# Expert weights as 8 KB runs per partition, with strided transposes to match

## The chip, the cores and the metric

The kernel runs on one core of a Trainium2 chip. The metric is the device time of one execution in microseconds; the time before is 1277.94 us, the median of three runs from 1277.46 to 1278.04.

## The reference, cut to what matters

One encoder block over 1024 tokens of width 1024, all in float32. A token mixer (multi-scale pooling and banded attention, gated and merged) and a layer norm come first and are not touched here. Then comes a mixture of experts: a router picks one of 4 groups and then 2 of its 8 experts for each token, so 2048 token rows are spread over 32 experts. For the rows `xb` of an expert `e`:

```python
hb = jax.nn.silu(xb @ w_gate[e]) * (xb @ w_up[e])      # [rows, 512]
y  = hb @ w_down[e]                                    # [rows, 1024]
```

`w_gate[e]` and `w_up[e]` are 1024 x 512, `w_down[e]` is 512 x 1024. The rows of `y`, weighted by the router, are added up per token, and a second layer norm closes the block. A matrix product sums over its inner index, so that index may be dealt out in any order, if both factors are dealt out alike.

## The kernel before, in words

TensorE multiplies over the partition axis, 128 values of the inner index at a time. Each float32 factor is split into a high and a low part in the format `float32r`, and a product is three matmuls: high by high, high by low, low by high (`mm3`, lines 94 to 98). Weights are the streamed operand, 512 columns wide; the transposed token rows are the loaded operand.

An expert's weights come as six chunks of 1 MB: `c` = 0, 1 are the halves of gate, 2, 3 those of up, 4, 5 those of down. `load_chunk` (line 980) reads a chunk into a tile `we` with a DMA that SyncE issues (GpSimd for a few early ones, of which some lie in parts in other tiles), line 995. `w_split` (line 999) makes the high part `weh` on ScalarE (line 1005) and the low part `wel` on VectorE (line 1007). The rows of weight are dealt out by `"(k p) c -> p k c"`: partition p holds the rows p, p + 128, p + 256 and so on, so a chunk brings four separate rows of 2 KB (gate, up) or two of 4 KB (down) to each partition.

The blocks of rows are 33 and have fixed sizes: four of 128 rows, 28 of the sizes in `CAPS` (the larger experts get the larger ones), and a second block of 64 rows for the largest expert:

```python
CAPS = [128]*5 + [112, 104, 104, 96, 96, 88, 80, 80] + [72]*4 + [64]*2 + [56]*3 + [48]*3 + [40]*2 + [32]
```

For a block, `gather` (line 1159) fetches its token rows into `xin` by an indirect DMA on GpSimd's queue, up to three blocks ahead. `x_transpose` (line 1165) turns them on TensorE, eight transposes of 128 columns into `xtp` in PSUM (line 1172); ScalarE and VectorE write the high and low parts into `xinT`. `chunk` (line 1177) does the matmuls of one weight chunk. After gate and up, `hidden` makes `h` (ScalarE, VectorE), and `h_transpose` (line 1204) turns `h` with four transposes into `htp` (line 1208), evicted into `hT`. `finish` scales `y` and adds it to DRAM by an indirect DMA on GpSimd's queue.

The order is written out by hand. `SEQ` holds for each block its chunks 0 to 3, and then chunks 4 and 5 of the block before it. After chunk 3 of a block TensorE turns the next block's rows, and after the following chunk 4 it turns `h`. `run_ahead` issues loads and splits as far ahead as buffers allow: 20 large buffers (`NBIG`) are shared by loaded chunks and their split parts, and splits run three to four chunks ahead. At the 12th block from the end, `overflow_setup` (line 1108) puts some thirty small operations on VectorE (line 1116 and on).

Of the kernel before, what the change touches and what calls it, by code (L numbers as in the profile page):

```python
# [33 lines left out]
EPS = 1e-5  # L34
OVF_MAX = 40          # nine experts have less than 64 rows, every other overflow block takes at least 65 of 2048 places
FIXED = 4             # experts whose places in the order don't depend on their counts
NV = NE - FIXED
CAP_UNIT = 8
CAPS = [128] * 5 + [112, 104, 104, 96, 96, 88, 80, 80] + [72] * 4 + [64] * 2 + [56] * 3 + [48] * 3 + [40] * 2 + [32]
SECOND = 64           # rows of the largest expert's second block  # L40
RANKS = S + 128
# [8 lines left out]
def kernel(  # L50
# [50 lines left out]

# [1 line left out]
    xh = [bigtile([128, 2, S], F32R, f"xh{j}") for j in range(4)]  # L103
# [35 lines left out]
    kT = [bigtile([128, NKV, S], F32R, f"kT{a}") for a in range(2)]  # L139
    # v's parts side by side, those of the second head the other way round  # L140
    vS = bigtile([128, NT, NKV, 2, HD], F32R, "vS")
# [24 lines left out]
    def rope_apply(t, i, n, tmp, eng=pool):  # L166
        # t = t * [cos cos] + swap(t) * [-sin sin], n heads of 64
        tv = t.rearrange("p (h a d) -> p h a d", h=n, a=2)
        sv = tmp.rearrange("p (h a d) -> p h a d", h=n, a=2)
        th = t.rearrange("p (h d) -> p h d", h=n)  # L170
        for a in range(2):
            eng.tensor_mul(sv[:, :, a, :], tv[:, :, 1 - a, :],
                            rope[:, i, 1, a * 32:(a + 1) * 32][:, None, :].to_broadcast([128, n, 32]))
        eng.tensor_mul(th, th, rope[:, i, 0, :][:, None, :].to_broadcast([128, n, HD]))
        eng.tensor_add(t, t, tmp)
# [49 lines left out]
    for h in range(2):  # L225
        sp.dma_start(wq[h], w_in[h * 512:(h + 1) * 512, 512:1024].rearrange("(k p) c -> p k c", p=128))
# [1 line left out]
    oh, ol, ob = [], [], []  # L228
# [8 lines left out]
    def q_proj(i, k):  # L237
        # one contraction tile of the query projection of block i
        if k == 0:
# [60 lines left out]
    def p_transpose(n):  # L300
        # one bank for two heads' first two key blocks, one for all heads' third
        b, h = divmod(n, NH)
# [12 lines left out]
    def p_evac(b, kv, q):  # L315
        # the q-th of the banks
        k0, k1 = krange(b)
# [23 lines left out]
    def o_evac(b, kv):  # L341
        # the sum over v's parts, the low part's half moved beside the high part's
        osb = ob[0]
        hi, lo = [slice(a * HD, (a + 1) * HD) for a in ((0, 1) if kv == 0 else (1, 0))]
        act.activation(osb[hi, 2 + kv], OP[b, kv][lo], AF.Copy)
        dve.tensor_add(osb[hi, b % 2], OP[b, kv][hi], osb[hi, 2 + kv])
# [54 lines left out]
    def hl_part(key, q):  # L401
        # a quarter of it
        if q == 0:
            RAW[key], WH[key] = WH[key], bigtile([128, 2, KT, 128], F32R, "ghl")
        raw, hl = RAW[key], WH[key]
        sl = slice(2 * q, 2 * q + 2)
        split(hl[:, 0, sl], hl[:, 1, sl], raw[:, sl])
# [4 lines left out]
    def gate_fill(n, k):  # L412
        # the first gate channels, where the last blocks leave the tensor engine free
        if k == 0:
# [13 lines left out]

    # the order of the steps before the first block, in turns of eight heads
    FIRST = {  # L430
# [10 lines left out]
    }  # L441
    # the order of a block's steps, in heads from its first head's turn
    ORDER = {
# [76 lines left out]

# [1 line left out]
    pb = ExitStack()  # L522
# [28 lines left out]
    def channels(key, half):  # L551
        # one 128-channel projection, channels on partitions, 512 tokens
        ps = gpp.tile([128, 512], F32, name="gps", bufs=3)
# [33 lines left out]
    def pool_window(j):  # L587
        # u is padded by eight zero columns on either side
        u = P["u", j]
# [3 lines left out]
        for s in range(j + 1):  # L593
            dst = gp.tile([128, W2], F32, name="wsum", bufs=2)
            # windows [t - d, t + d - 1] from two halves
            a, b_ = (1, 0) if s == 0 else (d // 2, d // 2)
# [30 lines left out]
    def project(s):  # L627
        # the channels of step s, for both halves of the tokens
        kind, j = steps[s]
# [68 lines left out]
    def routing_setup():  # L698
        # the slot table starts out with unused slots, their rows after those of the tokens
        trif = bigtile([128, 2, 128], F32, "trif")  # L700
# [53 lines left out]

# [1 line left out]
    pc = ExitStack()  # L756
# [23 lines left out]
    def logit_setup():  # L780
        # logits of LN(r): rstd * (r @ (g w)) - rstd * mean * (g @ w) + b @ w + bias
        dve.tensor_copy(eio, rc[0:1, 12:44])
# [11 lines left out]
    def rstd_of(r, v, t):  # L794
        # r = v ** -0.5 by Newton's method from a bit-level first guess, each step with its sign turned
        dve.tensor_scalar(v, v, EPS, 0.5, op0=ALU.add, op1=ALU.mult)
# [80 lines left out]
    def route_a(i):  # L877
        # choices and weights of token tile i
        lg = rp_.tile([128, 36], F32, name="lg")
# [9 lines left out]
        def first(x, m, rev, scr, k, h):  # L889
            # one-hot of the first position where x reaches m  # L890
            dve.scalar_tensor_tensor(scr, x, m, rev, op0=ALU.is_ge, op1=ALU.mult)
# [28 lines left out]
    def rank(i):  # L920
        # each expert's number times 1, its tokens so far times 32
        rk = rpp.tile([128, NE], F32, name="rk", bufs=1)
# [25 lines left out]

    # experts: the first FIXED in their order, the rest by their counts, RANK[p] the place among them
    RANK = {FIXED + q: r for q, r in enumerate(list(range(1, 7)) + [0] + list(range(7, NV)))}  # L950
# [3 lines left out]
    EXP = {p: p for p in range(FIXED)}  # L954
    # blocks in their order, with the expert place that each one's weights belong to
    BLOCKS = []
# [10 lines left out]
    for b, p, c in SEQ:  # L967
        if (p, c) not in LOADS:
            LOADS.append((p, c))
    # these two wait in buffers that the first blocks don't need yet  # L970
    GA = 3
# [4 lines left out]
    W = {}  # L976
    # the last chunks come in parts, the work on them follows sooner
    CUTS = {k: 2 for k in LOADS[-4:]}

    def load_chunk(key, e, eng=sp, aside=None):  # L980
        b, c = key
        if c < 4:
            src = (w_gate, w_up)[c // 2][e].rearrange("(k p) c -> p k c", p=128)[:, 4 * (c % 2):4 * (c % 2) + 4, :]
        else:
            src = w_down[e].rearrange("(k p) c -> p k c", p=128)[:, 2 * (c - 4):2 * (c - 4) + 2, :]
        n = src.shape[1]
# [79 lines left out]

# [1 line left out]
    tabv = tabd.rearrange("(r e) c -> r e c", e=NE)  # L1068
# [16 lines left out]
    novi = const.tile([128, 1], I32, name="novi")  # L1085
    # experts by their counts, the larger ones first
    sq = [128, NV, NV]
# [12 lines left out]

# [1 line left out]
    pd = ExitStack()  # L1102
# [5 lines left out]
    def overflow_setup():  # L1108
        # places of an expert past its static blocks go by 128, (j, e) the j-th such block of expert e
        rk = rk28  # L1110
# [22 lines left out]
    def overflow_next():  # L1133
        # the next overflow block's expert and its rows of the slot table
        v = mp.tile([128, 1], F32, name="ov", bufs=1)
# [13 lines left out]
    def place(b, p):  # L1149
        # the slots of a block  # L1150
        if p < FIXED:
# [12 lines left out]

    def x_transpose(b):
        n = ROWS[b]
        XT[b] = mp.tile([128, 2, KT, 128], F32R, name="xinT", bufs=1)
        for kk in range(2):
            ps = mpp.tile([128, 4, 128], F32, name="xtp", bufs=2)
            for c in range(4):  # L1170
                k = 4 * kk + c
                pe.transpose(ps[:, c, :n], XIN[b][:n, k * 128:(k + 1) * 128], ident[:n, :n])  # L1172
            split(XT[b][:, 0, 4 * kk:4 * kk + 4, :n], XT[b][:, 1, 4 * kk:4 * kk + 4, :n], ps[:, :, :n])
# [30 lines left out]
    def h_transpose(b):  # L1204
        n = ROWS[b]
        ps = mpp.tile([128, 4, 128], F32, name="htp")
        for c in range(4):
            pe.transpose(ps[:, c, :n], H[b][:n, c * 128:(c + 1) * 128], ident[:n, :n])
        HT[b] = mp.tile([128, 2, 4, 128], F32R, name="hT")
# [26 lines left out]
    for q in range(2, FIXED):  # L1236
        place(*BLOCKS[q])
    # how far the weights may be loaded and split ahead at each step
    last = {}
# [78 lines left out]

# [1 line left out]
    lp2 = ctx.enter_context(tc.tile_pool(name="lp2", bufs=2, reuse_waits="tile"))  # L1320
# [9 lines left out]
    def stats(i0):  # L1330
        mv = lp2.tile([128, 2, 8], F32, name="mv2", bufs=4)
        MV[i0] = mv
        for q in range(2):
            r = R[i0 + q]
            if i0 + q in ACT_STATS:
                # mean, and mean square about it
                junk = lp2.tile([128, D], F32, name="junk", bufs=1)
# [10 lines left out]
    def rstd2(i0):  # L1348
        # the root's reciprocal, and one Newton step
        mv = MV[i0]  # L1350
# [109 lines left out]
```

## Time and profile before

| what | value |
|---|---|
| median of the runs | 1277.94 us |
| profiled execution, first to last instruction | 1277.6 us |
| TensorE busy, matmul | 1186.8 us (93%) |
| TensorE busy, weight load | 887.1 us (69%) |
| VectorE busy | 907.3 us (71%) |
| ScalarE busy | 706.1 us (55%) |
| GpSimd busy | 288.7 us (23%) |
| transfers | 278.40 MB in 146391 packets |

PE is TensorE's matmul stream, PEld its weight loads, which can run beside it; DVE is VectorE, ACT ScalarE, POOL GpSimd, SPq the queue of SyncE. Matmuls are pipelined, so the busy time of a line is no measure of its pace: the distance from one start to the next is. The expert stage begins at 633 us, when the first gathered rows arrive, and ends at about 1222 us; the stretch before it holds the mixer, the first norm and the routing, the one behind it the second norm. PEclk 1.00 stands for a granted clock of 2.4 GHz, 0.5 for 1.2 GHz.

### The profile page before, as it was taken

How to read it: one execution, taken by the hardware profiler on the slowest of the kernel's cores; microseconds unless marked ns; L12 is line 12 of the kernel's file. 1: busy time of each engine (PE TensorE's matmuls, PEld its weight loads, DVE VectorE, ACT ScalarE, POOL GpSimd, SP SyncE). 2: the span in 40 equal slices, each digit the busy share in tenths (PEclk: the TensorE clock that was granted, in tenths of full speed). 3: DMA queues.
4: the chain of work that ended last, by engine and by line, in shares of the span. 5: the costliest groups of instructions: out<-in, count | busy, mean ns of one | idle time of the engine just before them, and what ended most of it. 6: DMA issues, size and time to landing. Idle time of an engine off the chain costs nothing.

```text
span 1277.6 us, 16403 instructions
## 1 busy us (share of the span) xinstructions
PE 1186.8 (93%) x5850; PEld 887.1 (69%) x5850; DVE 907.3 (71%) x1280; ACT 706.1 (55%) x933; POOL 288.7 (23%) x223
## 2 busy tenths in 40 slices
PE   8999999999999998998399999999999989999950
PEld 8888778888888887877278887767666645555520
DVE  5698962223742246898788999857988888888858
ACT  5578871111321141332377888757787767777733
POOL 3322200000000003566512222122221221222114
PEclk9999999999999998999599999999999989999985
DMA  7000113111111328448489999899999999999744
GB/s 266 1 2 1 44 34 118 40 45 42 53 55 50 116 74 283 135 133 296 161 313 370 376 376 375 294 335 380 327 373 376 371 398 356 375 387 387 288 136 176
DMA packets 146391, 278.40 MB, mean 218 GB/s; under 512 B 18948, under 2 KB 50692, under 8 KB 146308
## 3 DMA queue, kind: packets, MB, share of 16 engines
q1 hardware_dynamic: 137171, 249.00, 53.7%
q0 software_dynamic: 9136, 28.34, 8.4%
q8 instruction: 47, 0.77, 0.2%
q14 instruction: 37, 0.30, 0.1%
HBM read 251.83 MB, written 25.48 MB: 217 GB/s over the span
## 4 chain that ended last, share of the span: by engine, by line
PE 84%; DVE 10%; issue 2%; DMA 2%; ACT 1%; POOL 1%; SPq 0%; DVEq 0%; POOLq 0%; ACTq 0%
PE gps L98 5%; PE gps L96 5%; PE gps L97 5%; PE yp L96 5%; PE gate L98 5%; PE gate L97 5%; PE gate L96 5%; PE up L97 5%; PE up L96 5%; PE up L98 5%; PE yp L98 5%; PE yp L97 5%; PE yps L97 2%; PE yps L98 2%; PE yps L96 2%
## 5 line engine op out<-in xcount | busy, mean ns | idle before, releaser
L1007 DVE TENSOR_TENSOR wel<-we,weh 128x2048 fp32r<-128x2048 f32 (+1 forms) x193 | 426.7, 2245 | 73.6 <-ACT weh L1005 72.2
L1005 ACT ACTIVATE weh<-we 128x2048 fp32r<-128x2048 f32 (+1 forms) x193 | 355.2, 1876 | 21.2 <-PE up L97 10.0
L1221 POOL DMA_INDIRECT accd<-y,psl x29 | 71.2, 2455 | 384.0 <-ACT y L1220 303.7
L98 PE MATMUL gps<-xh,ghl 128*128 128x512 f32 x296 | 115.3, 390 | 0.0
L96 PE MATMUL gps<-xh,ghl 128*128 128x512 f32 x296 | 115.2, 389 | 0.0
L97 PE MATMUL gps<-xl,ghl 128*128 128x512 f32 x296 | 115.1, 389 | 0.0
L646 ACT ACTIVATE sig<-gps,bch 128x512 f32<-128x512 f32 x29 | 20.0, 689 | 168.8 <-PE gps L98 168.8
L97 PE MATMUL gate<-wel,xinT 128*128 128x512 f32 (+11 forms) x264 | 105.2, 399 | 5.2 <-DVE wel L1007 5.2
L96 PE MATMUL yp<-weh,hT 128*128 128x512 f32 (+11 forms) x264 | 107.7, 408 | 0.1
L96 PE MATMUL gate<-weh,xinT 128*128 128x512 f32 (+11 forms) x264 | 105.0, 398 | 0.8 <-ACT xinT L91 0.8
L98 PE MATMUL gate<-weh,xinT 128*128 128x512 f32 (+11 forms) x264 | 105.0, 398 | 0.2 <-DVE xinT L92 0.2
L98 PE MATMUL yp<-weh,hT 128*128 128x512 f32 (+11 forms) x264 | 103.8, 393 | 0.0
L96 PE MATMUL up<-weh,xinT 128*128 128x512 f32 (+11 forms) x264 | 103.8, 393 | 0.0
L97 PE MATMUL up<-wel,xinT 128*128 128x512 f32 (+11 forms) x264 | 103.7, 393 | 0.0
L97 PE MATMUL yp<-wel,hT 128*128 128x512 f32 (+11 forms) x264 | 103.6, 393 | 0.0
L98 PE MATMUL up<-weh,xinT 128*128 128x512 f32 (+11 forms) x264 | 103.5, 392 | 0.0
L92 DVE TENSOR_TENSOR ghl<-wraw,ghl 128x1024 fp32r<-128x1024 f32 (+1 forms) x26 | 26.4, 1020 | 82.5 <-ACT ghl L91 82.5
L91 ACT ACTIVATE xinT<-xtp 128x512 fp32r<-128x512 f32 (+11 forms) x66 | 26.9, 454 | 95.6 <-PE xtp L1172 95.6
L96 PEld LDWEIGHTS gps<-xh,ghl 128*128 128x128 f32 x296 | 55.6, 188 | 11.6
L97 PEld LDWEIGHTS gps<-xl,ghl 128*128 128x128 f32 x296 | 55.6, 188 | 11.6
L98 PEld LDWEIGHTS gps<-xh,ghl 128*128 128x128 f32 x296 | 55.6, 188 | 11.6
L97 PEld LDWEIGHTS gate<-wel,xinT 128*128 128x128 f32 (+11 forms) x264 | 40.8, 155 | 26.4 <-DVE wel L1007 5.7
(293 smaller groups left out, 2479.8 us busy)
## 6 DMA issues: line engine op xcount, KB each, us to landing
we<-in_w_gate_dram SPq DMA_DIRECT2D x62, 1024.0 KB, 10.1
we<-in_w_up_dram SPq DMA_DIRECT2D x61, 1024.0 KB, 13.3
we<-in_w_down_dram SPq DMA_DIRECT2D x60, 1024.0 KB, 14.9
wraw<-in_w_in_dram SPq DMA_DIRECT2D x20, 512.0 KB, 7.4
x<-in_x_dram SPq DMA_DIRECT2D x8, 512.0 KB, 8.8
wo<-in_w_o_dram SPq DMA_DIRECT2D x4, 1024.0 KB, 4.8
xr<-in_x_dram SPq DMA_DIRECT2D x8, 512.0 KB, 3.6
x1d<-r SPq DMA_DIRECT2D x8, 512.0 KB, 4.8
```

Source lines behind the costliest of these rows:

```text
L91: act.activation(hi, src, AF.Copy)
L92: dve.tensor_sub(lo, src, f(hi))
L96: pe.matmul(ps, lh, rh, start=first, stop=False)
L97: pe.matmul(ps, lh, rl, start=False, stop=False)
L98: pe.matmul(ps, ll, rh, start=False, stop=last)
L646: act.activation(dst[:, HALF[half]], ps, fn, bias=bch[:, bcol:bcol + 1])
L1005: act.activation(hi[:, sl], raw, AF.Copy)
L1007: dve.tensor_sub(lo[:, sl], raw, f(hi[:, sl]))
L1221: pool.indirect_dma_start(out=accd, out_offset=bass.IndirectOffsetOnAxis(ap=IDX[b][:n, 0:1], axis=0), in_=y[:n], in_offset=None, compute_o ...
```

## The change

The inner index of the expert products is dealt out as `"(p k) c -> p k c"`: partition p holds k consecutive rows of the matrix (8 of gate and up, 4 of down), and a chunk brings half of them, 8 KB that lie together. The transposes of `xin` and `h` pick their columns with the matching stride, so that partition p of the transposed rows holds the same index. The remaining lines of the diff are comments.

```diff
         if c < 4:
-            src = (w_gate, w_up)[c // 2][e].rearrange("(k p) c -> p k c", p=128)[:, 4 * (c % 2):4 * (c % 2) + 4, :]
+            src = (w_gate, w_up)[c // 2][e].rearrange("(p k) c -> p k c", p=128)[:, 4 * (c % 2):4 * (c % 2) + 4, :]
         else:
-            src = w_down[e].rearrange("(k p) c -> p k c", p=128)[:, 2 * (c - 4):2 * (c - 4) + 2, :]
+            src = w_down[e].rearrange("(p k) c -> p k c", p=128)[:, 2 * (c - 4):2 * (c - 4) + 2, :]
...
     def x_transpose(b):
         n = ROWS[b]
+        xk = XIN[b].rearrange("r (p k) -> r k p", k=KT)
...
-                pe.transpose(ps[:, c, :n], XIN[b][:n, k * 128:(k + 1) * 128], ident[:n, :n])
+                pe.transpose(ps[:, c, :n], xk[:n, k, :], ident[:n, :n])
...
     def h_transpose(b):
         n = ROWS[b]
+        hk = H[b].rearrange("r (p k) -> r k p", k=4)
         ps = mpp.tile([128, 4, 128], F32, name="htp")
         for c in range(4):
-            pe.transpose(ps[:, c, :n], H[b][:n, c * 128:(c + 1) * 128], ident[:n, :n])
+            pe.transpose(ps[:, c, :n], hk[:n, c, :], ident[:n, :n])
```

## Rows read from the trace of the kernel before

**Rows 1.** The page's first part: busy time, share of the span, instructions.
```profile
span 1277.6 us, 16403 instructions
...
PE 1186.8 (93%) x5850; PEld 887.1 (69%) x5850; DVE 907.3 (71%) x1280; ACT 706.1 (55%) x933; POOL 288.7 (23%) x223
```

**Rows 2.** Table by stretches of the span: start and end, length, engines' busy time.
```profile
core 0: us, PE busy (x) PEld busy (x) DVE busy (x) ACT busy (x) POOL busy (x), PEclk, DMA share, GB/s
...
662.00:1222.00 560.00, 554.83 (x2612) 368.47 (x2611) 474.54 (x337) 419.79 (x371) 128.27 (x62) 0.99 1.00 356
```

**Rows 3.** Waits of TensorE, 633 to 1232: total us, times, longest.
```profile
PE xtp L1172 <- DMA xin<-x1d,slots: 14.8, 1, 14.8
PE gate L97 <- DVE wel L1007: 5.2, 1, 5.2
PE gate L96 <- ACT xinT L91: 0.8, 1, 0.8
```

**Rows 4.** Matmuls in time order at three blocks' transposes: start, length, line, operands.
```profile
661.29 1.03 PE L1172 MATMUL xtp<-ident,xin 128*128 128x128 f32 x8
662.08 0.48 PE L96 MATMUL yp<-weh,hT 128*128 128x512 f32 x1
...
944.30 0.67 PE L1172 MATMUL xtp<-ident,xin 72*128 72x72 f32 x8
944.77 0.44 PE L96 MATMUL yp<-weh,hT 128*80 128x512 f32 x1
...
1013.98 0.71 PE L1172 MATMUL xtp<-ident,xin 64*128 64x64 f32 x8
1014.62 0.45 PE L96 MATMUL yp<-weh,hT 128*72 128x512 f32 x1
```

**Rows 5.** Weight loads in time order at two of these blocks.
```profile
661.06 1.02 PEld L1172 LDWEIGHTS xtp<-ident,xin 128*128 128x128 f32 x8
...
1013.98 0.57 PEld L1172 LDWEIGHTS xtp<-ident,xin 64*128 64x128 f32 x8 [0.42 <-issue]
```

**Rows 6.** Weight loads by line and shape, three of twelve shapes: busy us, mean ns.
```profile
L1172 PEld LDWEIGHTS xtp<-ident,xin 128*128 128x128 f32 x72 | 9.0, 149 | 16.0 <-DMA xin<-x1d,slots 14.9
...
L1172 PEld LDWEIGHTS xtp<-ident,xin 72*128 72x128 f32 x32 | 2.6, 141 | 0.7
...
L1172 PEld LDWEIGHTS xtp<-ident,xin 64*128 64x128 f32 x24 | 1.7, 138 | 1.2 <-issue 0.8 <-PE up L97 0.4
```

**Rows 7.** Matmuls in time order at the router's products, 506 to 509.
```profile
506.31 1.87 PE L873 MATMUL lp<-wg,x1T 128*128 128x36 f32 x16
508.01 0.48 PE L96 MATMUL z<-woh,mhl 128*128 128x512 f32 x1
```

**Rows 8.** VectorE's reductions by line and shape: count, busy us, mean ns.
```profile
L902 DVE TENSOR_REDUCE ro<-em 128x8 f32<-128x32 f32 x8 | 1.7, 215 | 0.3
L788 DVE TENSOR_REDUCE gsum<-wg 128x36 f32<-128x288 f32 x2 | 1.3, 666 | 0.1
...
L903 DVE TENSOR_REDUCE rw<-ro 128x1 f32<-128x8 f32 x8 | 1.3, 161 | 0.3
...
L1092 DVE TENSOR_REDUCE rk<-osq 128x28 f32<-128x784 f32 x1 | 1.0, 970 | 0.0
```

**Rows 9.** DMA queues, 662 to 1200: packets, MB, share of 16 engines.
```profile
DMA packets 82686, 195.83 MB, mean 364 GB/s; under 512 B 6382, under 2 KB 6382, under 8 KB 82650
...
q1 hardware_dynamic: 76378, 175.38, 86.6%
```

**Rows 10.** Waits of SyncE's queue, 633 to 1232: total us, times, longest.
```profile
SPq L995 <- DVE wel L1007: 111.8, 43, 18.3
```

**Rows 11.** Line 995, the loads, whole span: issue to landing.
```profile
DMA to landing us min/median/max: 6.0/10.6/18.2
```

**Rows 12.** Waits of ScalarE, 640 to 1232, for loads.
```profile
ACT weh L1005 <- DMA we<-in_w_down_dram: 0.7, 2, 0.5
```

**Rows 13.** VectorE in time order, 1014 to 1030: the overflow blocks' first operations.
```profile
1019.18 4.41 DVE L1116 SCALAR_TENSOR_TENSOR cap<-rk,cap 128x28 f32<-128x28 f32 x20
```

## The prediction

> **What bounds the kernel now.** I read the page's busy line first, then the table by stretches, then who waited for whom on TensorE, then the instructions around the edited lines in order of time, and last the DMA queues. TensorE is busy 93% of the span [rows 1]. The diff touches the expert stage only; from 662 to 1222 us TensorE is busy 554.8 of 560 us at a granted clock of 0.99 [rows 2]. Its waits in that stage are one for the first gathered rows (14.8 us, a gather, no weight load), one for the low half of a weight chunk (5.2 us) and 0.8 us for the first transposed rows [rows 3]. So a microsecond added to TensorE's own stream there comes out at the end, and one taken from a transfer comes out only where somebody waits for that transfer.
>
> **The loads.** Each 1 MB load of gate or up weights is today 128 partitions times four runs of 2 KB, each of down weights two runs of 4 KB; afterwards it is one run of 8 KB per partition. Bytes, number of issues and waits stay as they are. The transfer engines are not idle in this stage: share 1.00 at 356 GB/s [rows 2]; the weight queue alone holds 86.6% of the engines for 175.38 MB, in 76378 packets [rows 9]. A load takes 10.6 us in the median from issue to landing, up to 18.2 [rows 11], so several are queued. What hides it is the distance by which loads run ahead of their use: SyncE waits for a buffer to come free (111.8 us for VectorE's subtraction alone [rows 10]), which is a loader held back by its consumers, and the split on ScalarE waited for a load 0.7 us in the whole stage [rows 12]. I take the gain as 0. Bounds: at most those 0.7 us if the loads get faster; if they get slower, the cover goes after a few blocks (second rival). Should the runs not be merged into 8 KB, the time would be the same, since nothing rests on the gain.
>
> One rule speaks for a gain. The Trainium skill (Perfetto Trace Analysis, DMA Optimizations) says that going from 2 KB to 4 or 8 KB pieces can raise throughput much, for a kernel bound by its DMA at high memory use. By that rule alone the stage would shorten; the trace agrees on the high use (share 1.00) and not on the bound (0.7 us of waiting).
>
> **The transposes.** Contraction rows are now dealt to partitions in another order, so the transposes must pick every eighth column of `xin` (32 bytes apart in f32) and every fourth of `h` (16 bytes). Count, shapes, PSUM layout and all evictions stay. In these transposes the data is the operand that is loaded (LDWEIGHTS 128x128, 72x128, 64x128 [rows 6]) and the identity streams, so the strided read falls on the weight load. 33 blocks with 8 + 4 transposes make 396.
>
> What a load costs today: with 128 rows, eight transposes take 662.08 - 661.29 = 0.79 us; less some 0.03 us from the last start to the next matmul that is 7 steps of 109 ns. With 72 rows it is 944.77 - 944.30 = 0.47 us, steps of 63 ns. With 64 rows the eight loads take 0.57 us, the last one lasting 0.14, so steps of 62 ns again [rows 4, 5]. The step falls with the number of rows down to 62 ns and stays there: above it the identity's stream sets it (0.85 ns a column), at 72 rows and below the load of 128 columns. So a load needs 62 ns now, and at 128 rows 47 ns of lengthening would be hidden.
>
> No row shows TensorE reading with a stride. Bounds: nothing gets shorter than 62 ns, since shape and number of loads are the same, so the lower end is 0. The nearest strided reads are VectorE's reductions [rows 8]. Contiguous: (970 - 161)/(784 - 8) = 1.04 ns an element, with 153 ns fixed. At 32 bytes apart: (215 - 153)/32 = 1.94 ns. At 144 bytes apart: (666 - 153)/288 = 1.78 ns. So a stride of 32 bytes costs VectorE a factor 1.86. I take the factor: 62 x 1.86 = 115 ns a load. That lies near a load of the same form that this trace has: the sixteen f32 loads of line 873 step at 1.70/16 = 106 ns [rows 7]. For the upper end I take the absolute price, 1.94 ns for each of 128 columns = 250 ns.
>
> The Trainium skill (SBUF — State Buffer, Door 1: The DMA port swizzle, its note on cachelines) says that reads which step to a new 16-byte line each time lose speed, and that a line needs two hits or more to run at full rate. It names no price for TensorE. VectorE's rows agree with it (1.94 against 1.04 ns at 32 bytes); by it both strides here lose, by the factor or by the absolute price above.
>
> The sum at 115 ns. With more than 64 rows the first load of each group is hidden under the matmul before, so 7 + 3 = 10 steps a block count, at 0.85 ns a row today; block sizes are those of CAPS, with four blocks of 128 ahead of them:
> - 128 rows: 9 blocks x 10 x (115 - 109) = 0.5 us
> - 112, 104, 104, 96, 96, 88, 80, 80: steps are 95, 88, 82, 75 and 68 ns, so 10 x (20 + 27 + 27 + 33 + 33 + 40 + 47 + 47) ns = 2.7 us
> - 72: 4 x 10 x 53 ns = 2.1 us
>
> With 64 rows and fewer the loads start only with the group (the first of eight starts at 1013.98, as the group does [rows 4, 5]), so all 12 count: 12 blocks (with the second block of the largest expert) x 12 x 53 ns = 7.6 us.
>
> Together 13.0 us. At 106 ns it would be 10.1, at 250 ns 60.8 us: the same steps with 141 to 188 ns in place of 6 to 53.
>
> Nothing gives this back. The transposes stand in TensorE's own order between matmuls; the evictions behind them are used a chunk of matmuls later, and a delay of 0.2 to 0.6 us a block does not reach those. The 5.2 us wait ends with VectorE's queue, which holds 4.41 us of small operations for the overflow blocks [rows 13]; its chain starts behind the same transposes and moves with them. The profiled execution's span is 1277.6 us, and the median of the runs, 1277.94, lies 0.3 above. So 1277.6 + 0.3 + 13.0 = 1290.9 us.
>
> **Rivals.**
> - The weight load reads a strided column as fast as the next one. [...] Against it: VectorE's factor. Then nothing on the path changes: 1277.9 us. Chance 0.24.
> - The loads get slower: partitions now start 16 KB apart in DRAM, where rows that lay together were read by neighbouring partitions at once. It decides from a loss of about 2%, since the share is already 1.00 and the split has begun to wait for loads [rows 2, 12]. Place: the split on ScalarE, then TensorE's first matmul of a chunk. At 5% the 560 us stretch would want 28 us more; the loads would then set the pace, and the 13.0 us of the transposes would lie beneath: 1277.9 + 28 = 1306. Against it: the runs are longer. Chance 0.06.
> - The strided load pays the absolute price, 1.78 to 1.94 ns a column as on VectorE, thus 228 to 250 ns. Then it binds at every block size: 1277.9 + 53 to 61 = 1331 to 1339. For it: TensorE takes its columns faster than VectorE its elements (62/128 = 0.48 against 1.04 ns), so a price per access would weigh more. Against it: then even the 106 ns of [rows 7] would be far off. Chance 0.17.
> - Faster: reads without a price and an emptier DMA pull the splits forward, so that the 5.2 us wait goes: 1272.7. Against it: that wait ends with VectorE behind its own small operations, not with a load [rows 3, 13]. Chance 0.08.
>
> **How the numbers follow.** The forecast has 0.45, with its own range of 1286 to 1295 (loads of 100 to 125 ns, by the same steps). What a measurement here can tell from no change is about 0.2%, 2.6 us. The first rival gives "within" 0.24, the last one "faster" 0.08, the other cases "slower" 0.68. The range from 1276 to 1333 holds the forecast, the first rival, the slower loads and the lower part of the absolute price, and leaves out the faster case and the upper part: about 0.83 inside.
>
> **What would show it.** The step of the eight `xtp` loads: about 115 ns at 64 rows and fewer instead of 62, and hardly more than 109 at 128 rows. If it stays at 62, the first rival holds; at 200 or more, at 128 rows too, the absolute price. Weight packets should fall from 76378 to about a quarter to a third, the queue's share below 86.6%, SyncE's waits for buffers should grow, and TensorE's list of waits should not change. A wait of ScalarE or TensorE for `we` of more than a few us would show slower loads; the wait of 5.2 us gone would show the faster case. The prediction is wrong if the matmuls themselves change their step, or if the time moves with the transposes' steps unchanged.

## The result, and the profile after

| | median | runs | range |
|---|---|---|---|
| before | 1277.99 us | 4 | 1277.46 to 1279.06 |
| after | 1291.49 us | 4 | 1290.09 to 1291.61 |

The ratio is 1.0099 (95% interval 1.0085 to 1.0113), thus 10.9 to 14.4 us slower. The forecast was 1290.9 us.

The first part of the page after, and its line on transfers:

```profile
span 1289.5 us, 16403 instructions
...
PE 1197.5 (93%) x5850; PEld 900.3 (70%) x5850; DVE 909.9 (71%) x1280; ACT 707.1 (55%) x933; POOL 286.9 (22%) x223
...
DMA packets 91222, 278.40 MB, mean 216 GB/s; under 512 B 18947, under 2 KB 50691, under 8 KB 67459
```

Beside [rows 1], the counts of instructions are the same, the span is 11.9 us longer, TensorE's matmuls are busy 10.7 us longer and its weight loads 13.2. The other engines stay within 3 us of what they were. The bytes are the same; packets fell from 146391.

The expert stage after, in the table by stretches (columns as in [rows 2]; the stretch is 12 us longer for the same 2612 matmuls):

```profile
662.00:1234.00 572.00, 567.03 (x2612) 382.94 (x2611) 476.37 (x336) 420.33 (x370) 128.02 (x62) 0.99 0.95 348
```

TensorE still has no gaps to speak of (567.0 of 572 us) at the same granted clock of 0.99. So the 12 us are TensorE's own work that takes longer, not waiting. Its list of waits says the same (waited for: total us, times, longest; compare [rows 3]):

```profile
PE xtp L1174 <- DMA xin<-x1d,slots: 14.8, 1, 14.8
PE gate L97 <- DVE wel L1007: 5.0, 1, 5.0
PE gate L96 <- ACT xinT L91: 0.8, 1, 0.8
```

Where the time lies is seen at the transposes. Matmuls after, in time order: start, length, line, operands (they answer to [rows 4]; the last pair is `h` at 64 rows):

```profile
660.59 1.05 PE L1174 MATMUL xtp<-ident,xin 128*128 128x128 f32 x8
661.40 0.48 PE L96 MATMUL yp<-weh,hT 128*128 128x512 f32 x1
...
946.96 1.00 PE L1174 MATMUL xtp<-ident,xin 72*128 72x72 f32 x8
947.76 0.44 PE L96 MATMUL yp<-weh,hT 128*80 128x512 f32 x1
...
1018.68 1.09 PE L1174 MATMUL xtp<-ident,xin 64*128 64x64 f32 x8
1019.70 0.45 PE L96 MATMUL yp<-weh,hT 128*72 128x512 f32 x1
...
1048.63 0.69 PE L1211 MATMUL htp<-ident,h 64*128 64x64 f32 x4
1049.25 0.46 PE L96 MATMUL yp<-weh,hT 128*72 128x512 f32 x1
```

From the first start to the next product's start it is 0.81, 0.80 and 1.02 us for `xin`, where [rows 4] have 0.79, 0.47 and 0.64. Eight transposes no longer get cheaper as the rows get fewer: with 128 rows 0.02 us have come on top, with 64 rows 0.38 us. For `h` at 64 rows it is 0.62 us; the same place before:

```profile
1042.88 0.46 PE L1208 MATMUL htp<-ident,h 64*128 64x64 f32 x4
1043.27 0.45 PE L96 MATMUL yp<-weh,hT 128*72 128x512 f32 x1
```

That is 0.39 us, so 0.23 us more for four. And `h` at 128 rows, before and after:

```profile
664.90 0.60 PE L1208 MATMUL htp<-ident,h 128*128 128x128 f32 x4
665.26 0.48 PE L96 MATMUL yp<-weh,hT 128*128 128x512 f32 x1
```

```profile
664.24 0.63 PE L1211 MATMUL htp<-ident,h 128*128 128x128 f32 x4
664.63 0.48 PE L96 MATMUL yp<-weh,hT 128*128 128x512 f32 x1
```

Here four take 0.39 us in place of 0.36: at 128 rows most of the longer load is covered, for `h` not quite all of it. The weight loads after, at the 64-row block of 1018.68 and over the whole stage (by line: minimum, median and maximum ns of one; first and last start):

```profile
1018.68 0.96 PEld L1174 LDWEIGHTS xtp<-ident,xin 64*128 64x128 f32 x8 [0.41 <-issue]
...
L1174 PEld LDWEIGHTS xtp<-ident,xin x264: 182/202/230, 633.0 to 1212.8; 128*128 128x128 f32 x36, 72*128 72x128 f32 x16, 64*128 64x128 f32 x12, 56*128 56x128 f32 x12
```

Eight loads took 0.96 us where [rows 5] have 0.57. The length of one, some 200 ns, is not its pace, since the next starts within it: less the last one's 0.20 us these are 7 steps of 0.76/7 = 109 ns on average, against 62 before. Taken one by one, the first step of such a group is 91 ns and the others 110 to 113.

Last, the transfers, 662 to 1212 (packets, MB, share of the engines), and the queue of SyncE that issues the weights (waits as above):

```profile
DMA packets 32928, 195.73 MB, mean 356 GB/s; under 512 B 6389, under 2 KB 6389, under 8 KB 11730
...
q1 hardware_dynamic: 26620, 175.28, 81.9%
```

```profile
SPq L995 <- DVE wel L1007: 125.8, 53, 17.9
...
SPq L995 <- PE gate L98: 72.3, 26, 3.8
```

The weight queue moved the same MB [rows 9] in a third of the packets and held the engines for less (0.819 x 550 = 450 us in this stretch, against 0.866 x 538 = 466), and SyncE waited longer for buffers (125.8 us against 111.8 in [rows 10]; for the other row 72.3 against 52.5 before). The loads did get easier. Nobody had been waiting for them.

### The profile page after: what moved, and what is told of

It reads as the page before. It is cut to its first block, busy times and chain, and to the rows that moved or that the text cites. A ratio compares the mean times of both kernels' runs of the same rounds, so it can differ in the third digit from the quotient of the medians.

```text
span 1289.5 us, 16403 instructions
## 1 busy us (share of the span) xinstructions
PE 1197.5 (93%) x5850; PEld 900.3 (70%) x5850; DVE 909.9 (71%) x1280; ACT 707.1 (55%) x933; POOL 286.9 (22%) x223
## 4 chain that ended last, share of the span: by engine, by line
PE 84%; DVE 10%; DMA 2%; issue 2%; ACT 1%; POOL 1%; SPq 0%; DVEq 0%; POOLq 0%; ACTq 0%
PE gps L98 5%; PE gps L96 5%; PE gps L97 5%; PE yp L96 5%; PE gate L98 5%; PE gate L97 5%; PE gate L96 5%; PE up L97 5%; PE up L96 5%; PE up L98 5%; PE yp L98 5%; PE yp L97 5%; PE xtp L1174 2%; PE yps L97 2%; PE yps L98 2%; PE yps L96 2%
## 5 line engine op out<-in xcount | busy, mean ns | idle before, releaser
L92 DVE TENSOR_TENSOR ghl<-wraw,ghl 128x1024 fp32r<-128x1024 f32 (+1 forms) x26 | 26.4, 1019 | 82.7 <-ACT ghl L91 82.7
L98 PEld LDWEIGHTS gps<-xh,ghl 128*128 128x128 f32 x296 | 55.6, 188 | 11.7
```

The costliest lines, as they stand in the source:

```text
L92: dve.tensor_sub(lo, src, f(hi))
L98: pe.matmul(ps, ll, rh, start=False, stop=last)
```

## The experiments

The theory: each of the 396 strided weight loads takes about 115 ns in place of 62, that makes the time, and the runs of 8 KB are worth nothing. Its rivals: the loads' new order has a price or a gain of its own; and the price of the stride hangs on lines of 16 bytes, so that a stride of 8 bytes would be free. A ratio is to the kernel before on the same chip (1278.58 us for the first four, 1280.1 for the next four, 1279.37 for the last two).

**The loads alone.** The change with the old transposes; the rows and the weights then don't stand for the same index.

```diff
-                pe.transpose(ps[:, c, :n], xk[:n, k, :], ident[:n, :n])
+                pe.transpose(ps[:, c, :n], XIN[b][:n, k * 128:(k + 1) * 128], ident[:n, :n])
...
-            pe.transpose(ps[:, c, :n], hk[:n, c, :], ident[:n, :n])
+            pe.transpose(ps[:, c, :n], H[b][:n, c * 128:(c + 1) * 128], ident[:n, :n])
```

> The weights come in as 8 KB runs, the transposes read plain columns as in the kernel before (so rows and weights are no longer matched). Theory (the whole cost is the strided weight load of the transposes, the loads are hidden either way): 1278, within 2.6 us of the kernel before; eight transposes of 64 rows take 0.64 us from their first start to the next matmul, the weight queue's share falls to about 82% as in the changed kernel. Rival 1 (the new order of the loads costs part of the 13.5 us): 1281 to 1291. Rival 2 (the 8 KB runs gain time that the strides ate): below 1275.

Measured: 1279.46 us, ratio 1.0008 (0.9999 to 1.0017). The weight queue over the same stretch as in [rows 9] (662 to 1200), and TensorE's wait:

```profile
q1 hardware_dynamic: 26544, 175.14, 82.7%
```

```profile
PE gate L97 <- DVE wel L1007: 5.2, 1, 5.2
```

So 8 KB runs move the same MB for 82.7% of the engines against 86.6%, and the time does not follow. By the interval the new loads gain at most 0.1 us and cost at most 2.2, and the 5.2 us wait stays.

**The strides alone.** The change with the old loads (again not the same index):

```diff
-            src = (w_gate, w_up)[c // 2][e].rearrange("(p k) c -> p k c", p=128)[:, 4 * (c % 2):4 * (c % 2) + 4, :]
+            src = (w_gate, w_up)[c // 2][e].rearrange("(k p) c -> p k c", p=128)[:, 4 * (c % 2):4 * (c % 2) + 4, :]
...
-            src = w_down[e].rearrange("(p k) c -> p k c", p=128)[:, 2 * (c - 4):2 * (c - 4) + 2, :]
+            src = w_down[e].rearrange("(k p) c -> p k c", p=128)[:, 2 * (c - 4):2 * (c - 4) + 2, :]
```

> The transposes read strided columns, the weights come in as 2 and 4 KB runs as before (rows and weights are no longer matched). Theory: as slow as the changed kernel, 1290 to 1292, with steps of 110 ns for xin and 120 ns for h at 64 rows and fewer; loads stay hidden, since a slower TensorE gives them more time. Rival 1 (the loads cost part): clearly below 1290. Rival 2 (the runs gain): above 1293.

Measured: 1290.79 us, ratio 1.0092 (1.0077 to 1.0108). The loads of `xtp`, as above:

```profile
L1174 PEld LDWEIGHTS xtp<-ident,xin x264: 182/202/231, 634.0 to 1213.2; 128*128 128x128 f32 x36, 72*128 72x128 f32 x16, 64*128 64x128 f32 x12, 56*128 56x128 f32 x12
```

The whole change's ratio lies inside this interval. The strides are the loss: they cost 12.2 us by the medians, the loads alone 0.9 with an interval that takes in zero.

**Gate and up alone, down alone.** Two kernels that compute the reference: in one only gate, up and `xin` are changed (32 bytes), in the other only down and `h` (16 bytes).

```diff
 # only gate and up: these two lines as before
-            src = w_down[e].rearrange("(p k) c -> p k c", p=128)[:, 2 * (c - 4):2 * (c - 4) + 2, :]
+            src = w_down[e].rearrange("(k p) c -> p k c", p=128)[:, 2 * (c - 4):2 * (c - 4) + 2, :]
...
-            pe.transpose(ps[:, c, :n], hk[:n, c, :], ident[:n, :n])
+            pe.transpose(ps[:, c, :n], H[b][:n, c * 128:(c + 1) * 128], ident[:n, :n])
 # only down: instead the lines of gate, up and xin as before
```

> Only gate and up are dealt out anew and only xin is read with a stride (32 bytes); down and h as before. Theory: the xin transposes alone, which took 7.8 us longer in the changed kernel's trace: 1285.8, with h at 62 ns a step. If the two strides disturbed one another, the sum of this run's and the next one's cost would miss 12.5 us by more than 2.6.

> Only down is dealt out anew and only h is read with a stride (16 bytes); gate, up and xin as before. Theory: the h transposes alone, 4.7 us in the changed kernel's trace: 1282.7, with 120 ns a step. That a 16 byte stride costs more per load than a 32 byte stride (120 against 110 ns) should stay so here, if it belongs to the stride or to the tile and not to what runs beside it.

Measured: gate and up 1286.25 us, ratio 1.0059 (1.0045 to 1.0073), 7.7 us more; down 1282.59 us, ratio 1.0029 (1.0019 to 1.0040), 4.0 us more. Together 11.7 us, near the 12.2 of both strides at once, so neither disturbs the other. Added from start to start in the trace of the whole change, the transposes of `xin` take 7.7 us more and those of `h` 4.7. The loads of `htp` in the second kernel:

```profile
L1211 PEld LDWEIGHTS htp<-ident,h x132: 191/212/224, 653.4 to 1225.0; 128*128 128x128 f32 x36, 72*128 72x128 f32 x16, 64*128 64x128 f32 x12, 56*128 56x128 f32 x12
```

Half the stride is no cheaper: a load lasts 212 ns in the median against 202 for `xin`, and from the second load of a group on the step is 120 to 122 ns against 110 to 113.

**Smaller strides.** If a line of 16 bytes decided, two columns of f32 out of each line (8 bytes) would be enough. First, pairs of rows on a partition, so that both transposes step 8 bytes (the runs are 4 KB for gate and up, 8 KB for down); then four rows for `xin` (16 bytes) and two for `h` (8 bytes), all runs 8 KB. Both compute the reference.

```diff
-        xk = XIN[b].rearrange("r (p k) -> r k p", k=KT)
+        xk = XIN[b].rearrange("r (j p k) -> r j k p", p=128, k=2)
...
-                pe.transpose(ps[:, c, :n], xk[:n, k, :], ident[:n, :n])
+                pe.transpose(ps[:, c, :n], xk[:n, k // 2, k % 2, :], ident[:n, :n])
 # h in the same way; in the second kernel k=4, k // 4 and k % 4 for xin
 # load_chunk deals the weight rows out to match (not shown)
```

> Two rows that follow each other lie on one partition: gate and up come in as two runs of 4 KB per partition and chunk, down as one of 8 KB, and both transposes read every second column (8 bytes apart). Theory (a stride costs when each read steps to another 16 byte line of the partition; two f32 still share one at 8 bytes): steps of 62 ns as with plain columns, 1278 to 1280. Rival (any stride costs the load its second half, as 32 bytes did): steps of 110 to 120 ns, 1290 to 1292. A price that grows with the distance would lie between.

> The same 8 KB runs for all weights as in the changed kernel, other strides: xin is read at every fourth column (16 bytes), h at every second (8 bytes). Theory: h free, xin at a step of 110 to 122 ns. If the 120 ns of h in the changed kernel belong to the 16 byte stride, xin now steps at 116 to 122 and the time is 1288 to 1289.5; if they belong to the tile h, xin stays at 111 and the time is 1286. Rival of the run before (any stride costs): 1291 or more.

Measured: 1292.89 us, ratio 1.0103 (1.0086 to 1.0120), and 1293.23 us, ratio 1.0099 (1.0083 to 1.0116). A 64-row block of the first kernel:

```profile
1019.26 1.17 PE L1181 MATMUL xtp<-ident,xin 64*128 64x64 f32 x8
1020.37 0.46 PE L96 MATMUL yp<-weh,hT 128*72 128x512 f32 x1
```

It takes 1.11 us, more than the 1.02 at 32 bytes. And the loads of `xtp` in the first and in the second kernel:

```profile
L1181 PEld LDWEIGHTS xtp<-ident,xin x264: 190/214/231, 632.6 to 1213.5; 128*128 128x128 f32 x36, 72*128 72x128 f32 x16, 64*128 64x128 f32 x12, 56*128 56x128 f32 x12
```

```profile
L1175 PEld LDWEIGHTS xtp<-ident,xin x264: 191/214/226, 633.5 to 1214.9; 128*128 128x128 f32 x36, 72*128 72x128 f32 x16, 64*128 64x128 f32 x12, 56*128 56x128 f32 x12
```

The rival of the 16-byte line fell. At 8 bytes the step is 120 ns for `xin`, as at 16; and since `xin` and `h` agree at 16 bytes and at 8, the price belongs to the stride and not to the tile.

**Odd strides.** Were it banks that suffer from powers of two, 28 and 12 bytes would be cheaper. Other columns than the reference's are read here (896 of `xin`, 384 of `h`).

```diff
-        xk = XIN[b].rearrange("r (p k) -> r k p", k=KT)
+        xk = XIN[b][:, 0:896].rearrange("r (p k) -> r k p", k=7)
...
-        hk = H[b].rearrange("r (p k) -> r k p", k=4)
+        hk = H[b][:, 0:384].rearrange("r (p k) -> r k p", k=3)
...
```

> The changed kernel with other columns read: xin at every seventh (28 bytes), h at every third (12 bytes), so the columns picked are not those of the weights. Measured are the steps alone. So far 8 and 16 bytes stepped at 120 ns and 32 bytes at 111. If the longer stride is the cheaper one, 28 bytes steps near 111 to 113 and 12 bytes near 120; if powers of two are the matter, both fall away from 120 and 111; if each unit of distance had its price, 12 bytes lies between 62 and 120.

Measured: 1294.65 us in one run, against 1279.37 before. Loads of `xtp`:

```profile
L1174 PEld LDWEIGHTS xtp<-ident,xin x264: 193/218/226, 632.7 to 1216.0; 128*128 128x128 f32 x36, 72*128 72x128 f32 x16, 64*128 64x128 f32 x12, 56*128 56x128 f32 x12
```

It is 123 ns a step at 28 bytes, the dearest of all, and 113 to 120 at 12: little relief or none. A longer stride is thus not a cheaper one (28 bytes are above 120, not near 111), and the price does not grow with the distance either (12 bytes step faster than 8). The steps from start to start of single loads, at 64 rows and fewer and from the second load of a group on (the first step of a strided group is shorter, 90 to 100 ns), by stride in bytes, for 128 f32 columns:

| stride | 4 | 8 | 12 | 16 | 28 | 32 |
|---|---|---|---|---|---|---|
| `xin`, ns, mean | 62 | 120 | | 120 | 123 | 111 |
| `h`, ns, mean | 62 | 120 | 115 | 120 | | |

The price is that of leaving the next column, and within 8 to 32 bytes no order by distance is seen. That 32 bytes are 8% cheaper than 8 and 16 was seen in all traces of that stride, and 12 bytes lie between; why is open.

**Where loads do bind.** To see that the runs are worth something when they are waited for, two kernels leave out the two matmuls and the subtraction of the low parts (`mm3` becomes one matmul) and keep the old transposes; one has the old loads, the other the new (there the rows and the weights again don't stand for the same index).

```diff
+    def mm1(ps, lhs, rhs, first, last):
+        pe.matmul(ps, lhs[0], rhs[0], start=first, stop=last)
...
-            if low:
+            if low and False:
```

> The loads made the bound: of the three matmuls of a product in the expert stage only high by high is left, and the low parts of the weights are left out with VectorE's subtraction; loads in 2 and 4 KB runs and plain transposes as before. TensorE then needs some 7 us a block and ScalarE 15, the loads 17. Theory: the stage stays near 17 us a block, because the loads were just hidden: 1255 to 1275. If the loads had much room left, it would fall to ScalarE's 15 us a block, about 1200.

> As the run before, with 8 KB runs (and plain transposes, so rows and weights are not matched). Theory: where the loads bind, the runs show their gain: the weight queue took 86.6% of the engines for 175.38 MB before and 82.7% for 175.14 MB with 8 KB runs and plain transposes, 4.4% less, so 15 to 25 us faster than the run before. Rival (the order in DRAM gives nothing, or costs): within 5 us of it, or slower.

Measured: 1234.72 us (ratio 0.9646, 0.9627 to 0.9665) with the old loads and 1225.78 us (0.9576, 0.9557 to 0.9595) with the new. The first falls below what was expected for it: the loads had more room left than the share of 1.00 in [rows 2] suggests. The gain of the new loads, 8.9 us, has the expected sign and about half the size. The stretch from 662 to 1150 in the kernel before, then with the old loads and with the new (columns as in [rows 2]), the last two with ScalarE's waits for loads:

```profile
662.00:1150.00 488.00, 482.83 (x2282) 332.30 (x2281) 413.31 (x296) 366.87 (x322) 116.20 (x57) 0.99 1.02 362
```

```profile
662.00:1150.00 488.00, 327.33 (x1031) 171.34 (x1032) 64.27 (x142) 384.86 (x337) 70.33 (x60) 0.65 1.05 375
```

```profile
ACT weh L1005 <- DMA we<-in_w_gate_dram: 63.0, 45, 4.2
ACT weh L1005 <- DMA we<-in_w_down_dram: 23.6, 45, 3.0
ACT weh L1005 <- DMA we<-in_w_up_dram: 18.9, 24, 2.8
```

```profile
662.00:1150.00 488.00, 315.93 (x1046) 166.16 (x1046) 64.59 (x143) 392.84 (x344) 72.60 (x61) 0.69 1.02 382
```

```profile
ACT weh L1005 <- DMA we<-in_w_gate_dram: 55.3, 42, 4.5
ACT weh L1005 <- DMA we<-in_w_down_dram: 21.8, 28, 3.3
ACT weh L1005 <- DMA we<-in_w_up_dram: 18.6, 24, 2.1
```

In the full kernel these waits are 0.7 us [rows 12]; here they add up to 105.5 and 95.7 us (633 to 1190), and the 9.8 us between them are close to the 8.9 us of time. The transfers run at 375 GB/s and 382, where the kernel before takes 362 in the same stretch.

**The 5.2 us wait.** The last rival let it go by faster loads; the prediction held that it ends with VectorE's small operations for the overflow blocks [rows 13]. On the kernel before, without the change, these operations are handed out one per weight chunk from the 12th block from the end on:

```diff
     def overflow_setup():
...
+        yield                      # after each operation
...
-                overflow_setup()
+                OVS.append(overflow_setup())
...
+        if OVS:
+            next(OVS[0], None)     # one at each chunk
...
+    for _ in OVS[0]:
+        pass
```

> The kernel before (2 and 4 KB runs, plain transposes), with the some thirty small operations for the overflow blocks handed out one at each weight chunk over the last 12 blocks, in place of all at once on VectorE. Theory (TensorE's wait of 5.2 us for a low half is VectorE behind these operations, no load): the wait goes, and with it the half clock that follows it; 12 matmuls stepped at 0.43 in place of 0.23 us, 2.4 us; 1278 - 7.6 = 1270.5. Rival (the loads, which ran with no lead left at that point, would make the wait anyway): 1275 to 1278, with a wait of ScalarE for we in its place.

Measured: 1271.69 us (1270.81 to 1272.45), ratio 0.9937 (0.9923 to 0.9951). That is 7.7 us faster than the kernel before. TensorE's waits, the whole of the list above 0.2 us:

```profile
PE xtp L1184 <- DMA xin<-x1d,slots: 14.9, 1, 14.9
PE gate L96 <- ACT xinT L91: 0.8, 1, 0.8
```

The wait is gone, but the gain is 2.5 us more than it. The kernel before, in time order at this wait, and in the table by stretches:

```profile
1028.81 0.69 PE L97 MATMUL gate<-wel,xinT 128*64 128x512 f32 x1 [5.17 <-DVE wel L1007]
...
1029.72 0.63 PE L96 MATMUL gate<-weh,xinT 128*64 128x512 f32 x1
1030.14 0.63 PE L97 MATMUL gate<-wel,xinT 128*64 128x512 f32 x1
...
1034.62 0.40 PE L97 MATMUL up<-wel,xinT 128*64 128x512 f32 x1
1034.85 0.39 PE L98 MATMUL up<-weh,xinT 128*64 128x512 f32 x1
```

```profile
1010.00:1023.60 13.60, 13.60 (x67) 8.11 (x65) 11.35 (x26) 9.67 (x11) 0.70 (x5) 1.00 1.05 367
1023.60:1028.80 5.20, 0.03 (x1) 0.00 (x0) 5.00 (x10) 4.50 (x3) 2.40 (x2) 0.83 1.07 401
1028.80:1033.50 4.70, 4.70 (x11) 2.52 (x12) 4.70 (x3) 0.69 (x1) 0.00 (x0) 0.50 1.03 338
```

After 5.2 us without work TensorE got 0.50 of its clock (1.2 GHz) for 4.7 us, and its matmuls stepped 0.43 us in place of 0.23: eleven of them, 11 x 0.20 = 2.2 us. With the wait's 5.2 that is 7.4 us, near the 7.7 measured. In the new kernel the clock is 1.00 over all of 1010 to 1050:

```profile
1010.00:1050.00 40.00, 40.00 (x188) 23.68 (x186) 35.66 (x32) 28.92 (x26) 9.73 (x7) 1.00 1.05 376
```

## Why the prediction was right, step by step

**What bounds.** Right. TensorE's stretch grew by what its instructions grew; its waits did not move.

**The loads, 0.** Right in the balance: 0.9 us by themselves, an interval from -0.1 to 2.2. The signs named for it came: weight packets at 35% of before (a quarter to a third had been named), the queue's share down, SyncE's waits up. The second rival (slower loads, 1306) fell with the loads alone. Its point of decision, a loss of about 2%, was too tight as well: with TensorE's work cut down the same loads ran at 375 GB/s, 3.6% above the 362 of the same stretch before. A DMA share of 1.00 was thus not the end of what they can do. The rule of the Trainium skill (Perfetto Trace Analysis, DMA Optimizations), that larger pieces help a kernel bound by its DMA, holds with its condition: 8.9 us where the loads are waited for, nothing where TensorE sets the pace. The gain it calls large was small here: 382 GB/s in place of 375.

**The step, 62 to 115 ns.** Right in kind and size: 111 ns for `xin`, 120 for `h`, one a little below and one a little above. It was a choice, VectorE's factor from [rows 8], and it was near by more luck than reason: VectorE's factor belongs to 32 bytes, and TensorE pays the like at 8, where no row had been read. The 106 ns of [rows 7], which the prediction found near, are loads without a stride and say nothing of one. The rival without a price and the one with the absolute price (228 to 250 ns) are both excluded by each trace after. The price of a strided load is close to a doubling of the step (62 to about 120 ns, at 32 bytes to 111).

**The sum, 13.0 us.** From the start before to the start after each group of transposes, against the same blocks of the kernel before, the traces give 12.45 us: 0.45 at 128 rows (predicted 0.5), 2.57 at 112 to 80 (2.7), 2.02 at 72 (2.1), 7.41 at 64 and fewer (7.6). At 64 rows and fewer two misses partly cancel, which is luck: a group of `xin` took 385 ns more where 8 x 53 = 424 were counted, a group of `h` 233 where 4 x 53 = 212 were. The span grew 11.9 us and the medians 13.5; the interval of the ratio covers both and the 13.0. What carried most was that the identity's stream covers the longer load at 128 rows and covers less with each row fewer: without it the 128-row blocks would have paid 9 x 12 x 53 ns = 5.7 us and not 0.5.

**The rule on lines.** The Trainium skill (SBUF — State Buffer, Door 1: The DMA port swizzle, its note on cachelines) lets two accesses to a 16-byte line run at full rate. On TensorE's weight loads here it does not hold: 120 ns at 8 bytes against 62 contiguous. The measurement decides. The rule gave the right sign for this change, but it would have advised the 8-byte version, which is as slow.

**The faster rival.** Its gain is real (the wait can go, and more than 5.2 us with it), its cause was wrong: no load stood behind it, since the 8 KB loads left the wait at 5.2 us. That is as the prediction argued against it. That the time behind the wait is lost too, at half the clock, its price of 5.2 us did not have.

## What to carry to other kernels

Before making a transfer's runs longer, look whether anyone waits for it, and price what the new layout does to the operand that must follow it: here a unit stride given up in 396 weight loads cost 12 us, and 8 KB runs returned nothing. Price an instruction by the distance between starts and by what covers it at each size, not by its own duration. And a wait of TensorE costs more than its length where the granted clock falls behind it.

## What the runs showed of the hardware

- A weight load of 128 f32 columns steps 62 ns with contiguous columns and 111 to 123 ns on average at the strides measured, 8, 12, 16, 28 and 32 bytes. A stride of 8 bytes (120) is hardly better than 28 (123); 32 bytes are the cheapest (111). The cause of that is open.
- With 128 rows the step of a transpose is 109 ns by the identity's stream, and it covers nearly all of the longer load: eight transposes of `xin` took 0.81 us for 0.79, four of `h` 0.39 for 0.36.
- 8 KB runs on a partition take 82.7% of the engines for MB that took 86.6% in 2 and 4 KB runs.
- After 5.2 us of idleness TensorE ran 4.7 us at a granted clock of 0.50 (1.2 GHz).
- With one matmul in place of three for each product, the granted clock from 662 to 1150 us was 0.65 to 0.69 in place of 0.99 (1031 and 1046 matmuls in place of 2282). What that cost those two kernels was not measured.
